# Four-layer diffusion backbone on one core: where the last layer's conditioning products run

## The chip, the core and the metric

The kernel runs on one core of a Trainium2 chip. Five engines work on instruction streams of their own: TensorE (PE, matmuls and transposes), VectorE (DVE), ScalarE (ACT), GpSimd (POOL) and SyncE (SP, which here only issues DMA transfers). Engines wait for one another by semaphores, and DMA queues move data between device memory and the on-chip buffers. The metric is device time in microseconds of one execution, as the median of several.

## The reference

Four layers run one after the other over 384 tokens: 128 context tokens and 256 latent tokens, each of width 1024. Layers 0 and 3 are S5 state-space mixers, layer 1 is a pooling mixer, layer 2 is latent attention (MLA). Each layer is normed, shifted and scaled by its conditioning, mixed, multiplied with a SiLU path z, projected back and added to the residual with a conditioned gate:

```python
def _ada(cond, w, b):
    m = jax.nn.silu(cond) @ w + b            # (1024) @ (1024, 3072)
    return jnp.split(m, 3, axis=-1)
for layer in range(4):
    sh, sc, g = _ada(c, ada_w[layer], ada_b[layer])    # and the same for c_ctx
    h = _rmsnorm(x, norm_g[layer]) * (1 + sc) + sh
    u, z = jnp.split(h @ w_in, 2, axis=-1)             # MLA: z beside q, ckv, kpe
    y = mixer(u)                                       # S5: scan over the tokens, then GLU
    x = x + g * ((y * silu(z)) @ w_out)
```

The conditioning (shift, scale and gate of every layer) depends on the two vectors c and c_ctx alone, so its products may run at any time before the layer that uses them.

## The kernel before

**Conditioning.** Each of the 4 layers has three parts: shift (part 0), scale (part 1) and gate (part 2). A part is a product of the two condition vectors with a 1024 x 1024 block of ada_w. `ada_steps` (from line 82) cuts a part into four steps. A step loads two 512 KB pieces of weights, `adw`, over SP's queue, and TensorE multiplies each piece in four fp32 matmuls on 32 columns (line 99), which the trace shows as 8 records. So a part is 8 loads and 64 records. The loads go into a ring named "araw" with two buffers (layer 0's shift and scale also use another ring). The sums stay in one PSUM bank, `adps`, of the pool `ad`, which has a single bank that other work shares. The last step adds the bias on VectorE (`adarow`, line 51 through a helper); then shift and scale are transposed on TensorE (`adt`, line 111) and written by ScalarE or VectorE, and a gate is stored by four small transfers (`gd`).

**Order of the parts.** `program` keeps all 48 steps in a list `todo`, in order of layer and part; `fill()` takes the next four, which is one part. Layer 0's shift and scale are done before its scan. The other ten parts, 40 steps with 80 loads, are all handed out in layer 0's scan.

**First scan (layer 0, `S5Body.run`).** The S5 layer works in four blocks b of channels. Per block TensorE makes the inputs u (line 213), chunk products (line 1122), a recurrence over time steps runs on VectorE (tiles Pr, E, R at line 51), ScalarE copies the states (`Eq`, lines 1185 and 1188, 2.9 us each), and TensorE makes the outputs from them (lines 1208 and 1212). z products of layer 0 (line 204) and the parts of the conditioning fill TensorE beside the recurrence; the lines are

```python
for k in range((3, 4, 3, 6)[b]):
    at(62, self.z, zs.pop(0))
if fill:
    for k in range((4, 3, 2, 1)[b]):
        at(45, fill)
```

so the four blocks get 4, 3, 2 and 1 parts: 32, 24, 16 and 8 loads.

**Attention layer (layer 2).** Its projection has 16 z products (`zprod`), each 24 matmuls of a 512 KB weight (lines 159 to 161), which ScalarE and VectorE first split in two (`whi` line 138, `wlo` line 51). After each, `side(1, 1)` is called: its first number runs one task of preparation of layer 3's tables (`S5Ahead`, which makes its tables P and t in the ring "araw" as well, and stores and loads them over SP), its second calls `fill(1)`, which finds `todo` empty.

**Later scan (layer 3, `S5Skewed.run`).** The same work in five phases f, with the tables loaded instead of made (`Wl`, ring "araw", asked for in phases 0 to 2), and its z products in three matmuls per tile (lines 159 to 161). The second half of the GLU work (lines 829 to 831) comes behind it.

**What sets the order.** The code hands instructions to a scheduler that arranges each engine's stream anew by when operands come ready, so the streams differ from the order of the code; each engine then runs its stream in order. A wait holds up all that stands behind it on the same engine or queue.

Of the kernel before, what the change touches and what calls it, by code (L numbers as in the profile page):

```python
# [9 lines left out]
F32 = mybir.dt.float32  # L10
# [20 lines left out]
class Net:  # L31
# [51 lines left out]
    def ada_steps(self, l, g):  # L83


        nc, m = self.nc, self.mods[l]
        st = {}

        def load(ks):
            if 0 in ks:  # L90
                st["ps"] = self.ad.tile([128, 256], F32, name="adps", tag="ad")
                st["row"] = self.load(self.work, self.A["ada_b"][l, g], [128, 256], "adarow", bufs=1)
            ps, first = st["ps"], l == 0 and g < 2
            for k in ks:
                tag = "raw" if first and k % 3 else "araw"
                raw = self.ring.tile([128, 4, 256], F32, name="adw", tag=tag, bufs=4 if tag == "raw" else 2)
                nc.sync.dma_start(raw, self.A["ada_w"][l, g, k])
                for h in range(4):
                    nc.tensor.matmul(ps[32 * h:32 * h + 32, :], self.scond[:, k, :], raw[:, h, :], start=k == 0, stop=k == 7)  # L99
            if 7 in ks:  # L100
                finish(ps, st["row"])

        def finish(ps, row):
            self.tt(row, ps, row, OP.add)
            if g == 2:
                for h in range(4):
                    nc.sync.dma_start(m["gd"][:, h * 256:(h + 1) * 256], row[32 * h:32 * h + 2, :])
                return
            pt = self.ad.tile([128, 2, 4, 32], F32, name="adt", tag="ad")
            for k in range(2):  # L110
                nc.tensor.transpose(pt[:, k].rearrange("p h c -> p (h c)"), row[:, k * 128:(k + 1) * 128], self.ident)
            pv = pt[:, :, :, 0:2].rearrange("p k h c -> p h k c")
            if g == 0:
                nc.scalar.copy(out=m["sh"].rearrange("p (h k) c -> p h k c", k=2), in_=pv)
            else:
                for k in range(2):
                    nc.vector.scalar_tensor_tensor(out=m["sc"][:, k::2, :], in0=pt[:, k, :, 0:2], scalar=1.0,
                                                   in1=self.gT[:, l, k::2].unsqueeze(2).broadcast_to([128, 4, 2]),
                                                   op0=OP.add, op1=OP.mult)

        return [lambda ks=range(i, i + 2): load(ks) for i in range(0, 8, 2)]
# [910 lines left out]
class S5Body:  # L1032
# [198 lines left out]
    def run(self, h, fill, glu):  # L1231
        self.h = h

        self.Es = [p.tile([128, 99, 64], F32, name="E", tag="e") for p in (self.eps[0], self.e1)]
        self.Ps, self.Ms = {}, {}
        self.u(0)
        for qq in range(4):
            self.win(0, qq)
        zs = list(range(16))
        for b in range(4):  # L1240
            tasks = {}
            at = lambda i, f, *a: tasks.setdefault(i, []).append(lambda: f(*a))
            if b < 3:
                at(4, self.u, b + 1)
            for qq in range(4):
                if b < 3:
                    at(8 + 14 * qq, self.win, b + 1, qq)
                at(6 + 14 * qq, self.mats, 4 * b + qq)
            for k in range((3, 4, 3, 6)[b]):
                at(62, self.z, zs.pop(0))  # L1250
            if fill:
                for k in range((4, 3, 2, 1)[b]):
                    at(45, fill)
            if b == 3:
                for q in range(8):
                    at(min(62, 30 + 6 * q), glu.early_y, self.wq, q)
                for q in zs:
                    at(62, self.z, q)
                for q in range(2):
                    at(62, glu.early_prod, q)  # L1260
            self.rec(b, tasks)
            for qq in range(4):
                q = 4 * b + qq
                self.out(b, qq)
                if b == 3:
                    for k in range(2, 6):
                        if (0, 1, 2, 3, 3, 3)[k] == qq:
                            glu.early_prod(k)
                if qq < 2:
                    self.Ms[q + 2] = self.m_mat(q + 2)  # L1270
        self.nc.sync.dma_start(self.A["o_s5"][self.j], self.fin.rearrange("p q g r -> p (q g r)"))


class S5Skewed(S5Body):
# [17 lines left out]
    def run(self, h, fill, glu):  # L1292
# [7 lines left out]
        for f in range(5):  # L1300
# [9 lines left out]
            for k in range((2, 4, 4, 5, 1)[f]):  # L1310
                at(14 + 3 * k, self.z, zs.pop(0))
            if f == 3:
                for q in range(8):
                    at(8 + 3 * q, glu.early_y, self.wq, q)
            if f == 4:
# [24 lines left out]
def program(tc, A, layers=(0, 1, 2, 3), final=True):  # L1340
    with ExitStack() as ctx:
# [28 lines left out]
        for l in layers:  # L1370
            n = [0, 0]

            def side(k, a):
                n[0] += k
                n[1] += a
                while ahead and n[0] >= 1:
                    ahead.side()
                    n[0] -= 1
                while n[1] >= 1:
                    fill(1)  # L1380
                    n[1] -= 1

            def end():
# [150 lines left out]
```

## Time and profile before

| | us |
|---|---|
| median of 3 runs | 1811.44 (1811.34 to 1813.9) |
| profiled execution, its own time | 1812.23 |
| its span | 1810.4 |
| TensorE busy in it | 1686.1 (93%) |
| mean granted TensorE clock | 0.963 of full |

The page gives the busy time of each engine and the chain of work that ended last. Other views cut the same execution finer: windows (busy time per engine in a stretch), waits (what ended the idle time of an engine), the chain in order of time, and timelines of single instructions, in which a number in brackets is the idle time before an instruction and what ended it. A row with x8 stands for 8 records of the same shape, back to back or overlapping, so the step from its start to the next row's start is what it holds the engine for.

### The profile page before, as it was taken

Reading aid. Unit: us, or ns where it says so; the run is one execution under the profiler, and the core shown is the slowest. Engines: PE = TensorE matmul, PEld = TensorE weight load, DVE = VectorE, ACT = ScalarE, POOL = GpSimd, SP = SyncE. Lnnn points to the kernel's source line nnn. Section 1 sums busy time; section 2 is a strip of 40 time slices with the busy share of each in tenths; the row PEclk is TensorE's granted clock in tenths of the full one; section 3 lists DMA queues with packets and bytes.
Section 4 is the critical chain, followed back from the end, with each engine's and each line's share of the span. In section 5 each row is a group of like instructions: output and inputs, shape, how many; then the busy total and the mean of one; then the engine's idle time right before and its main releaser. Section 6 shows DMA issues by size and latency. Waiting matters only on the chain.

```text
span 1810.4 us, 29493 instructions
## 1 busy us (share of the span) xinstructions
PE 1686.1 (93%) x10928; PEld 1318.4 (73%) x10928; DVE 1254.9 (69%) x3149; ACT 978.3 (54%) x1588; POOL 5.4 (0%) x16
## 2 busy tenths in 40 slices
PE   4999999998999998999998999999899999899998
PEld 1464454654799977999887885657678778689986
DVE  7699876787476567888867737763439978656435
ACT  2653487636654455655546555642354777754322
POOL 0000000000000000000000000000000000000000
PEclk7999999997899998999998999999999999799999
DMA  8337767654577664655563566732567754567552
GB/s 311 98 119 240 228 182 220 195 180 137 166 252 231 193 205 135 188 162 163 179 218 113 186 205 229 239 127 82 181 226 226 227 182 140 166 232 213 172 165 72
DMA packets 174831, 334.30 MB, mean 185 GB/s; under 512 B 78528, under 2 KB 101856, under 8 KB 174688
## 3 DMA queue, kind: packets, MB, share of 16 engines
q1 hardware_dynamic: 165728, 319.84, 55.6%
q10 hardware_dynamic: 8960, 12.59, 2.1%
q8 instruction: 86, 1.41, 0.3%
q14 instruction: 57, 0.47, 0.1%
HBM read 279.54 MB, written 52.82 MB: 184 GB/s over the span
## 4 chain that ended last, share of the span: by engine, by line
PE 72%; DVE 9%; ACT 9%; DMA 6%; issue 3%; SPq 0%; ACTq 0%; DVEq 0%
PE acc L175 6%; PE acc L177 6%; PE acc L176 6%; PE sp L1122 4%; PE acc L829 4%; PE acc L830 4%; PE acc L831 4%; PE acc L213 3%; PE acc L159 3%; PE acc L160 3%; PE acc L161 3%; PE acc L204 3%; ACT Eq L1188 3%; DMA adw<-in_ada_w 2%; PE adps L99 2%
## 5 line engine op out<-in xcount | busy, mean ns | idle before, releaser
L51 DVE TENSOR_TENSOR wlo<-raw,whi 128x1024 fp32r<-128x1024 f32 (+2 forms) x234 | 281.2, 1204 | 246.3 <-ACT whi L138 229.0
L138 ACT CAST whi<-raw 128x1024 fp32r<-128x1024 f32 x246 | 257.6, 1050 | 315.2 <-PE acc L177 130.0
L51 DVE TENSOR_TENSOR Pr<-E,Tb 128x256 f32<-128x256 f32 (+1 forms) x504 | 173.9, 354 | 9.3 <-ACT E L1131 3.3
L159 PE MATMUL acc<-hh,whi 128*128 128x384 f32 x512 | 177.3, 347 | 0.2
L161 PE MATMUL acc<-hh,wlo 128*128 128x384 f32 x512 | 174.3, 340 | 0.3 <-DVE wlo L51 0.2
L160 PE MATMUL acc<-hl,whi 128*128 128x384 f32 x512 | 174.3, 340 | 0.0
L829 PE MATMUL acc<-y,whi 128*128 128x384 f32 x448 | 152.7, 345 | 8.1 <-ACT y L146 5.8
L831 PE MATMUL acc<-y,wlo 128*128 128x384 f32 x448 | 152.0, 340 | 1.0 <-DVE wlo L51 1.0
L830 PE MATMUL acc<-y,whi 128*128 128x384 f32 x448 | 152.7, 342 | 0.1
L175 PE MATMUL acc<-whi,ph 128*128 128x512 f32 x384 | 152.5, 397 | 0.0
L176 PE MATMUL acc<-wlo,ph 128*128 128x512 f32 x384 | 151.4, 394 | 0.0
L177 PE MATMUL acc<-whi,pl 128*128 128x512 f32 x384 | 151.3, 394 | 0.0
L51 DVE TENSOR_TENSOR E<-R,E 128x128 f32<-128x128 f32 (+1 forms) x504 | 123.1, 254 | 31.5 <-ACT E L1125 25.2
L51 DVE TENSOR_TENSOR R<-Pr 128x128 f32<-128x128 f32 (+1 forms) x504 | 123.7, 255 | 5.8
L159 PEld LDWEIGHTS acc<-hh,whi 128*128 128x128 f32 x512 | 97.1, 190 | 5.2 <-issue 2.0
L204 PE MATMUL acc<-h,raw 128*128 128x384 f32 x256 | 98.8, 516 | 0.0
L161 PEld LDWEIGHTS acc<-hh,wlo 128*128 128x128 f32 x512 | 96.8, 189 | 2.1 <-DVE wlo L51 0.9
L160 PEld LDWEIGHTS acc<-hl,whi 128*128 128x128 f32 x512 | 97.1, 190 | 1.0 <-issue 0.3
L99 PE MATMUL adps<-adw,scond 128*32 128x256 f32 x768 | 70.6, 422 | 27.7 <-DMA adw<-in_ada_w 27.3
L213 PE MATMUL acc<-raw,h 128*128 128x512 f32 x192 | 95.8, 617 | 0.0
L829 PEld LDWEIGHTS acc<-y,whi 128*128 128x128 f32 x448 | 84.6, 190 | 11.6 <-ACT y L146 7.1
L831 PEld LDWEIGHTS acc<-y,wlo 128*128 128x128 f32 x448 | 84.9, 190 | 2.2 <-DVE wlo L51 1.6
(285 smaller groups left out, 3261.6 us busy)
## 6 DMA issues: line engine op xcount, KB each, us to landing
adw<-in_ada_w SPq DMA_DIRECT2D x96, 512.0 KB
raw<-in_s_glu SPq DMA_DIRECT2D x64, 512.0 KB
raw<-in_s_wu SPq DMA_DIRECT2D x48, 512.0 KB
raw<-in_s_wz SPq DMA_DIRECT2D x40, 512.0 KB
raw<-in_s_wo SPq DMA_DIRECT2D x32, 512.0 KB
yq<-yd SPq DMA_DIRECT2D x64, 192.0 KB
lod<-wlo SPq DMA_DIRECT2D x24, 512.0 KB
wlo<-lod SPq DMA_DIRECT2D x24, 512.0 KB
```

Of the source, the lines that this page charges most:

```text
L51: return self.nc.vector.tensor_tensor(out=out, in0=a, in1=b, op=op)
L138: nc.scalar.copy(out=hi, in_=raw)
L159: nc.tensor.matmul(ps, h, xh[:, kk, :ncol], start=i == 0, stop=False)
L160: nc.tensor.matmul(ps, h, xl[:, kk, :ncol], start=False, stop=False)
L161: nc.tensor.matmul(ps, l, xh[:, kk, :ncol], start=False, stop=i == n - 1)
L175: nc.tensor.matmul(ps, xh[:, kk, xs], h, start=kk == 0, stop=False)
L176: nc.tensor.matmul(ps, xh[:, kk, xs], l, start=False, stop=False)
L177: nc.tensor.matmul(ps, xl[:, kk, xs], h, start=False, stop=kk == 2 * nu - 1)
L204: self.nc.tensor.matmul(ps, w[:, k * 128:(k + 1) * 128], x[:, k, :], start=k == 0, stop=k == 7)
L829: self.nc.tensor.matmul(ps, h, y[:, 0, k], start=u == 0 and k == 0, stop=False)
L830: self.nc.tensor.matmul(ps, h, y[:, 1, k], start=False, stop=False)
L831: self.nc.tensor.matmul(ps, l, y[:, 0, k], start=False, stop=u == 1 and k == 7)
```

## The change

The last layer's three parts leave the first scan. The blocks now get 3, 2, 2 and 0 parts (24, 16, 16 and 0 loads). Shift and scale of layer 3, eight steps with 16 loads, are handed out one step after each of the first eight z products of the attention layer. The gate, four steps with 8 loads, is handed out in phase 3 of the later scan, and it sums in a bank of the pool `sp` instead of `ad`.

```diff
@@ ada_steps
         def load(ks):
             if 0 in ks:
-                st["ps"] = self.ad.tile([128, 256], F32, name="adps", tag="ad")
+                st["ps"] = (self.ad.tile([128, 256], F32, name="adps", tag="ad") if (l, g) != (3, 2) else
+                            self.bank(self.sp, "sp")[:, :256])
@@ S5Body.run
             if fill:
-                for k in range((4, 3, 2, 1)[b]):
+                for k in range((3, 2, 2, 0)[b]):
                     at(45, fill)
@@ S5Skewed.run
             if f == 3:
+                at(4, fill)
                 for q in range(8):
                     at(8 + 3 * q, glu.early_y, self.wq, q)
@@ program, side
                 while n[1] >= 1:
-                    fill(1)
+                    if l == 2 and todo and todo[0][:2] <= (3, 1):
+                        fill(1)
                     n[1] -= 1
```

Lines of the changed kernel are one higher from line 92 on (two from 1315, three from 1383): its line 100 is line 99 of before. The streams of the two kernels show the moves. In the next pieces a load of adw is one row with x4, its four matmuls.

TensorE, first scan, end of the first block: `L204` are layer 0's z products, `L1208` and `L1212` the block's outputs from the state copies Eq, `L214` (changed) the next block's inputs u. Before:

```order
L99 MATMUL adps<-adw,scond 32x256 x4
L204 MATMUL acc<-h,raw 128x384 x2
L99 MATMUL adps<-adw,scond 32x256 x4
L204 MATMUL acc<-h,raw 128x384 x3
L1212 MATMUL tp<-Eq,P 64x96 x4
L99 MATMUL adps<-adw,scond 32x256 x4
L1208 MATMUL tp<-U_608,M 128x96
L1212 MATMUL tp<-Eq,P 64x96 x4
```

Four more such loads stand in the eight rows ahead of it. Changed, at the same place:

```order
L112 MATMUL adt<-ident,adarow 128x128 x2
L214 MATMUL acc<-raw,h 128x512
L1209 MATMUL ad<-U_608,M 128x96
L214 MATMUL acc<-raw,h 128x512 x2
L205 MATMUL acc<-h,raw 128x384 x19
L1213 MATMUL tp<-Eq,P 64x96 x4
L1209 MATMUL tp<-U_608,M 128x96
L1213 MATMUL tp<-Eq,P 64x96 x4
```

These loads are gone, and 19 z matmuls stand together ahead of the first output.

SP's queue, layer 2's z products: `raw<-in_mla_wz` are the z weights; lfq, C, W, Td, Md, Pd and Wd are tables of layer 3's preparation. Before:

```order
L136 DMA raw<-in_mla_wz 128x1024
L1001 DMA Md_590<-W 128x512
L946 DMA Td_5190<-Tt 128x112
L55 DMA lfq<-Lfd_591 128x64
L136 DMA raw<-in_mla_wz 128x1024 x2
L991 DMA Wd_588<-W 128x1024
L994 DMA Pd_589<-P 128x1024
L136 DMA raw<-in_mla_wz 128x1024
```

Changed:

```order
L995 DMA Pd_589<-P 128x1024
L98 DMA adw<-in_ada_w 128x1024
L137 DMA raw<-in_mla_wz 128x1024
L98 DMA adw<-in_ada_w 128x1024
L947 DMA Td_5021<-Tt 128x112
L137 DMA raw<-in_mla_wz 128x1024 x3
L55 DMA adarow<-in_ada_b 128x256
L55 DMA lfq<-Lfd_591 128x64
L98 DMA adw<-in_ada_w 128x1024 x2
L992 DMA Wd_588<-W 128x1024
L137 DMA raw<-in_mla_wz 128x1024
```

Loads of adw and of the bias (adarow) now stand among the z weights and the preparation's transfers.

TensorE, later scan, phase 3: `L1208`, `L1212` (before) and `L1209`, `L1213` (changed) are the outputs from Eq, `L159` to `L161` (changed: `L160` to `L162`) the z products. Before:

```order
L1208 MATMUL tp<-U_12635,M 128x96
L1212 MATMUL tp<-Eq,P 64x96 x4
L1208 MATMUL ad<-U_12635,M 128x96
L159 MATMUL acc<-hh,whi 128x384
L160 MATMUL acc<-hl,whi 128x384
L161 MATMUL acc<-hh,wlo 128x384
L159 MATMUL acc<-hh,whi 128x384
```

Changed:

```order
L1209 MATMUL tp<-U_12579,M 128x96
L1213 MATMUL tp<-Eq,P 64x96 x4
L1209 MATMUL ad<-U_12579,M 128x96
L100 MATMUL sp<-adw,scond 32x256 x8
L160 MATMUL acc<-hh,whi 128x384
L161 MATMUL acc<-hl,whi 128x384
L162 MATMUL acc<-hh,wlo 128x384
```

Two loads (x8) of the gate stand ahead of the z matmuls that follow an output group; three more such pairs follow further down, the last of them 94 rows on, so that z matmuls move behind later outputs.

## Rows read from the trace of the kernel before

**Rows 1.** The page, parts 1 and 4.

```profile
PE 1686.1 (93%) x10928; PEld 1318.4 (73%) x10928; DVE 1254.9 (69%) x3149; ACT 978.3 (54%) x1588; POOL 5.4 (0%) x16
...
PE 72%; DVE 9%; ACT 9%; DMA 6%; issue 3%; SPq 0%; ACTq 0%; DVEq 0%
```

**Rows 2.** Windows: us; busy us of each engine (x instructions), granted clock, DMA share, GB/s.

```profile
90.00:457.00 367.00, 339.49 (x2836) 189.49 (x2832) 297.69 (x980) 211.11 (x309) 0.30 (x2) 0.96 0.60 187
...
1020.00:1080.00 60.00, 60.00 (x358) 55.77 (x351) 26.42 (x34) 30.62 (x51) 0.00 (x0) 1.00 0.64 201
1500.00:1600.00 100.00, 87.69 (x622) 74.73 (x621) 75.55 (x253) 75.84 (x62) 0.00 (x0) 0.90 0.54 177
```

**Rows 3.** Windows of the tile adps alone, first scan: PE, PEld, DVE, clock, DMA, GB/s.

```profile
90.00:457.00 367.00, 56.50 (x640) 15.42 (x640) 4.23 (x10) 0.96 0.60 187
```

**Rows 4.** TensorE's waits in the first scan: for whom, us, times, longest.

```profile
PE tp L1212 <- ACT Eq L1188: 9.9, 4, 4.5
PE adps L99 <- DMA adw<-in_ada_w: 8.5, 8, 2.4
```

**Rows 5.** Chain that ended last, shares by line: 90 to 460, then 430 to 460 us.

```profile
by line: PE acc L204 14.4%; PE acc L213 11.8%; PE sp L1122 10.4%; DMA adw<-in_ada_w 10.1%; PE adps L99 10.0%; ACT Eq L1188 6.2%; issue 5.2%; PE sp L910 3.2%; PE ad L1212 3.2%; ACT Eq L1185 3.1%; PE sp L938 2.8%; DVE Pr L51 2.5%; PE ad L1208
...
by line: PE acc L204 43.8%; DMA adw<-in_ada_w 15.9%; PE adps L99 14.5%; ACT Eq L1188 9.5%; PE tp L1212 5.7%; PE sp L938 4.2%; PE tp L1208 3.3%; ACT sz L1095 1.7%; ACTq L1097 1.1%; issue 0.8%; ACTq L1188 0.1%
```

**Rows 6.** Windows of shorter stretches, columns as in rows 2.

```profile
150.00:200.00 50.00, 47.56 (x294) 19.87 (x286) 43.97 (x191) 4.31 (x11) 0.00 (x0) 1.00 0.80 254
...
360.00:390.00 30.00, 29.98 (x175) 15.55 (x173) 28.38 (x139) 2.42 (x5) 0.00 (x0) 1.00 0.76 253
400.00:410.00 10.00, 10.00 (x74) 6.77 (x73) 3.21 (x6) 8.33 (x7) 0.00 (x0) 0.66 0.10 30
...
1080.00:1100.00 20.00, 18.31 (x76) 11.39 (x75) 16.44 (x40) 13.94 (x27) 0.00 (x0) 1.00 0.84 294
```

**Rows 7.** TensorE's timeline, first block's end: start, length, instruction, idle before.

```profile
205.83 0.64 PE L99 MATMUL adps<-adw,scond 128*32 128x256 f32 x8 [1.39 <-DMA adw<-in_ada_w]
...
209.17 0.64 PE L99 MATMUL adps<-adw,scond 128*32 128x256 f32 x8
209.74 1.56 PE L204 MATMUL acc<-h,raw 128*128 128x384 f32 x4
```

**Rows 8.** TensorE's timeline, fourth block, as rows 7.

```profile
435.96 1.08 PE L99 MATMUL adps<-adw,scond 128*32 128x256 f32 x8 [2.39 <-DMA adw<-in_ada_w]
436.97 4.21 PE L204 MATMUL acc<-h,raw 128*128 128x384 f32 x6
...
457.31 0.55 PE L1212 MATMUL tp<-Eq,P 128*64 128x96 f32 x8 [2.42 <-ACT Eq L1188]
```

**Rows 9.** Chain in order of time: start, length, what.

```profile
187.25 4.64 DMA adw<-in_ada_w
...
211.05 2.92 ACT Eq L1188
...
333.56 6.22 DMA adw<-in_ada_w
```

**Rows 10.** ScalarE's timeline beside the z products.

```profile
1056.42 1.05 ACT L138 CAST whi<-raw 128x1024 fp32r<-128x1024 f32 x1 [2.72 <-PE acc L160]
...
1060.58 1.05 ACT L138 CAST whi<-raw 128x1024 fp32r<-128x1024 f32 x1 [2.72 <-PE acc L160]
```

**Rows 11.** TensorE's timeline, layer 2: first transposes, last z product's end.

```profile
961.63 0.66 PE L267 MATMUL sp<-ident,xn 128*128 128x128 f32 x2 [4.31 <-issue]
...
1072.86 0.33 PE L161 MATMUL acc<-hh,wlo 128*128 128x384 f32 x1
```

**Rows 12.** TensorE's timeline, later scan.

```profile
1535.23 0.55 PE L1212 MATMUL ad<-Eq,P 128*64 128x96 f32 x8 [1.49 <-ACT Eq L1188]
...
1561.94 0.69 PE L829 MATMUL acc<-y,whi 128*128 128x384 f32 x1 [3.43 <-ACT y L146]
```

**Rows 13.** TensorE's timeline, third block's end.

```profile
399.52 0.55 PE L1212 MATMUL tp<-Eq,P 128*64 128x96 f32 x8 [3.00 <-ACT Eq L1188]
```

## Prediction, written before the changed kernel ran

> **What bounds the kernel now.** I read the page first. TensorE is busy 93% of the span and holds 72% of the chain that ended last [rows 1], so an instruction taken off TensorE counts wherever no other engine is just behind it, and one put on TensorE costs its full time wherever TensorE has no gap. The change moves work between three stretches, so the table by stretch comes next [rows 2]. In the first scan (90 to 457 us) TensorE is busy 339.49 of 367 us, VectorE 297.69 and ScalarE 211.11. In the stretch with the attention layer's z products (1020 to 1080) TensorE is busy 60.00 of 60, VectorE only 26.42. In the later scan (1500 to 1600) TensorE is busy 87.69 of 100 and ScalarE 75.84.
>
> The moved work is the conditioning. In the first scan its matmuls are 640 records, 80 loads of 8, 56.50 us busy [rows 3]. TensorE waits there for two things above all: 9.9 us for ScalarE's Eq copies and 8.5 us for conditioning weights (adw) [rows 4]. The chain says the same from the other side: 10.0% of the 370 us are adps matmuls and 10.1% adw transfers, 74 us together [rows 5]. So this stretch is mostly bound by TensorE's order and by its loads, with ScalarE second, and VectorE close in places (43.97 of 50 us at 150 to 200 us) [rows 6].
>
> **First scan: 24 of 80 loads leave.** By the blocks of the scan the loads go from 32, 24, 16, 8 to 24, 16, 16, 0. What one load costs on the path is the start of its 8 records to the start of the next matmul: 209.17 to 209.74, 0.57 us [rows 7]; at the low clock, 435.96 to 436.97, 1.01 us [rows 8]. The first 16 loads at 0.57 are 9.1 us. The last 8, of the fourth block, begin at the low clock and end at the high one; I take 0.75 each, between the two, 6.0 us. Waits that go with them: 1.39 us at 205.83 [rows 7], 2.39 us at 435.96 [rows 8], and of the rest a share, 8 of the 24 loads of the second block, about 1.3 us of those in [rows 4]. Sum 9.1 + 6.0 + 5.1 = 20.2 us.
>
> Not all of it comes out. At 208 to 219 us the chain runs on ScalarE's Eq copies (2.92 us each, [rows 9]) and not on TensorE; there the freed time is only filled by z products moved up from below, which is what the order shows for the first block's end. That pays later if TensorE is the limit later, which it is at 360 to 390 (29.98 of 30) [rows 6]. In the fourth block the chain goes over adw, adps and the z matmuls (15.9%, 14.5% and 43.8% of 30 us [rows 5]) into the Eq copy that TensorE waits for until 457.31 [rows 8], so there the relief is on the path. I take **-17 us**. The bounds: -8 (only the fourth block, 6.0 + 2.4) and -20.
>
> **z products: 16 loads are added.** One z product is 4.16 us (the weight split for one starts at 1056.42, for the next at 1060.58 [rows 10]), all of it TensorE, so 16 loads at 0.57 add 9.1 us. By the order the first two stand before layer 2's first transposes, where TensorE is idle 4.31 us [rows 11], and that gives back 2 x 0.57 = 1.1 us. Then the waits. A load's buffer comes free when TensorE has read it, the ring has two, and a round trip takes 4.64 us (187.25) to 6.22 us (333.56) [rows 9]. In the order the four loads from the third of the scale part on stand 9 or 10 z matmuls apart; two gaps and a load are 20 x 0.173 + 0.57 = 4.0 us (0.173 = 4.16 / 24), so a wait of 0.6 to 2.2 us comes up at two or three of them. At the densest place of the first scan (150 to 200 us) 18 loads left TensorE idle for 50 - 47.56 = 2.4 us [rows 6]. Here the DMA engines also carry the z weights (512 KB per 4.16 us, 126 GB/s) and layer 3's preparation, 201 GB/s in all [rows 2]. The loads stand from the idle at 961 to 82 z matmuls (14 us) before the last one at 1072.86 [rows 11]; 16 of 0.524 MB over these 98 us add 86 GB/s and make 287, about what the busiest slices show (294 GB/s at 1080 to 1100 [rows 6]). I take 3 us of waits: 9.1 - 1.1 + 3.0 = **+11 us**. Bounds: +8 (no wait) and +17 (every second load waits about 1.1 us). What queues behind: on TensorE the next z matmul; on SP the z weights and the preparation's stores, issued in order behind a load that waits for its buffer; on VectorE, behind the two adarow additions, which wait for a part's last load, the splits of z weights that TensorE reads next. VectorE has 33 of 60 us free here.
>
> The Trainium skill, "DMA: Bandwidth & Descriptors", section "Anatomy of one DMA", fits a transfer, for GpSimd's path, as about 2 us fixed plus its bytes over 436 GB/s. As an estimate from that page a 512 KB load takes 3.2 us, where the trace shows 4.64 to 6.22 for these loads of SP's queue; by the page the waits beside the z products would vanish and their term would be +8 instead of +11. The measured rows decide, so I keep +11.
>
> **Later scan: 8 loads are added.** 8 x 0.5 to 0.57 us is 4 to 4.6 us. They stand before ScalarE's Eq copies, where TensorE idles 1.49 us, with 3.43 us further on for y [rows 12]; they take the place of z matmuls, which slide into those gaps. The cover is ScalarE, 75.84 of 100 us [rows 2]. I take **+0.5 us**; without the cover it is +4.6, with one wait for a load (2.4 us, as at 435.96) +7; and -1 if the slid z matmuls fill gaps so that the clock, 0.90 over this stretch [rows 2], rises a little. The accumulator takes one of the two sp banks, but no other sp matmul stands between these loads in the order, so nothing waits for it. The four gd stores and adarow are the same in number as before.
>
> **Sum.** -17 + 11 + 0.5 = -5.5 us. Of the profiled run, 1812.23 us, that leaves 1806.7; the median shown is 0.8 us below the profiled run, so **1806.0 us**.
>
> **Rivals.**
> A, the first scan gives little. ScalarE's Eq copies and VectorE's recurrence (28.38 of 30 us at 360 to 390 [rows 6]) hold the scan where TensorE gets shorter. For it: the 9.9 us [rows 4]; against it: the 74 us of [rows 5]. The relief is then 9 to 13 us, the rest as above, net +2.5 to -1.5: 1810 to 1814, no measurable change.
> B, **slower**: the z products starve. The loads share SP, ring and DMA engines with the z weights and the preparation, which here are already at 201 GB/s; the ring's other users, the preparation's own tables, lengthen the round trip to the 6.22 us seen. If 8 of the 14 loads wait 1.3 us each, that is 10 us. Idle time of some us has cost clock in this trace: TensorE idled 3.00 us before 399.52 [rows 13], and from 400 to 410 us the granted clock is 0.66 [rows 6], a mix of its two levels, 2.4 and 1.2 GHz. One such 10 us here costs 3 to 4 us. Then z is +9.1 - 1.1 + 10 + 3 = +21, net +4.5 to +8 with a first scan of -17 to -13.5: 1816 to 1819. It decides from about 9 us of waits in the z stretch. For it: adw is what TensorE waits for in the first scan too, 8 times [rows 4], with no z weights beside it; against: from 1020 to 1080 TensorE has no gap at all at 201 GB/s [rows 2].
> The Trainium skill, "TensorE: Matmul & The Clock Gate", section "Part 1: The HAM clock gate", says that the engine is throttled unless it is kept active; the row at 399.52 agrees, and that is why B carries the clock term.
> C, all comes out: -20 in the first scan, its end at a higher clock too, z at +8, later scan -1: -13, 1798.
> D, the move changes what the scheduler does elsewhere so that gain and cost cancel (the order below the moved loads differs on all queues): about 1811.
>
> **Chances.** The forecast 0.38 (gain of 3.6 to 10 us, 1801 to 1807.8), A 0.22, B 0.25, C 0.08, D 0.07. A measurement of this kernel tells 0.2%, 3.6 us, from no change. Faster is forecast and C, 0.46; same is A and D, 0.29; slower is B, 0.25. The range reaches from half of C to two thirds of B: 1799 to 1819 leaves out about 0.04 + 0.08, and some 0.05 for sizes beyond all bounds.
>
> **What would show it.** In the changed profile: 56 loads of adw in 90 to about 440 us, no TensorE wait for adw near 205 and 435, and the scan's last copy 15 us earlier or more. Right in size if the layer 3 preparation's stretch (first transposes of layer 2 to the attention scores) is 9 to 13 us longer with at most 4 us of waits for adw. Wrong if TensorE's waits for Eq in the first scan grow from 9.9 us by over 8 (rival A), or if waits for adw or z weights near 1000 to 1060 exceed 9 us or the clock there falls below 1.00 (rival B). The later scan should hold its time within 1 us from layer 3's first Eq copy to its last.

## The result and the profile after

The changed kernel takes 1838.37 us (median of 4 runs, 1834.54 to 1838.95), the kernel before 1811.85 beside it: a ratio of 1.014, 95% interval 1.0124 to 1.0157. It is slower by 26.5 us, outside the range of 1799 to 1819. The profiled run took 1834.54 us with a span of 1832.6, 22.3 more than the profiled run of before; the comparisons of stretches below are of these two executions.

The page after, parts 1 and 4, against [rows 1] (from here on lines of the changed kernel are numbered one to three higher, as the change section says):

```profile
PE 1696.7 (93%) x10928; PEld 1325.2 (72%) x10928; DVE 1248.7 (68%) x3149; ACT 977.6 (53%) x1588; POOL 5.4 (0%) x16
...
PE 69%; DVE 10%; ACT 9%; DMA 8%; issue 3%; SPq 0%; ACTq 0%; DVEq 0%
```

TensorE is busy 10.6 us more, and its share of the last chain falls from 72% to 69% while the DMA's rises from 6% to 8%. Of the 22.2 us that the span grew, 10.6 are thus longer busy time for the same 10928 records, and 11.6 are idle time of TensorE. Windows after, columns as in [rows 2]:

```profile
90.00:457.00 367.00, 328.93 (x2655) 190.88 (x2651) 297.32 (x986) 214.10 (x314) 0.30 (x2) 0.92 0.52 156
1020.00:1080.00 60.00, 57.51 (x389) 47.90 (x388) 25.61 (x37) 25.98 (x46) 0.00 (x0) 1.00 0.73 226
1500.00:1600.00 100.00, 91.95 (x754) 77.69 (x753) 78.38 (x268) 78.09 (x74) 0.00 (x0) 0.94 0.63 204
```

In the first scan's 367 us TensorE is busy 328.93 us against 339.49, so it did get lighter. But VectorE is busy 297.32 against 297.69 us, and TensorE's granted clock fell from 0.96 to 0.92. Where TensorE got its time back it waited. Its waits after, in the stretch of [rows 4]:

```profile
PE tp L1213 <- ACT Eq L1189: 22.0, 4, 11.8
PE adps L100 <- DMA adw<-in_ada_w: 5.6, 11, 1.0
```

The wait for Eq is 22.0 us where it was 9.9. The wait for adw shrank from 8.5 to 5.6. What was taken off TensorE came back as waiting for ScalarE's copies. These in turn wait for the last step of VectorE's recurrence (`E`). ScalarE's timeline shows it for the third block, before and then after:

```profile
393.73 2.89 ACT L1185 COPY Eq<-E 64x1536 f32<-64x1536 f32 x1 [17.70 <-DVE E L51]
```

```profile
395.01 2.83 ACT L1186 COPY Eq<-E 64x1536 f32<-64x1536 f32 x1 [0.51 <-DVE E L51]
```

In the kernel before too, ScalarE stood idle until the recurrence was done, 17.70 us there. With less work on TensorE the recurrence ended no earlier. In the timeline of TensorE, and in a window of the stretch:

```profile
400.72 0.91 PE L1213 MATMUL tp<-Eq,P 128*64 128x96 f32 x8 [11.76 <-ACT Eq L1189]
```

```profile
395.00:430.00 35.00, 23.12 (x160) 16.93 (x163) 21.94 (x69) 28.59 (x18) 0.00 (x0) 0.50 0.10 29
```

The first wait was 3.00 us before [rows 13]; it is 11.76 now, and over this window the granted clock is 0.50, the lower of its two levels (1.2 GHz), where the same window had 0.68 before and 400 to 410 had 0.66 [rows 6].

How far the changed kernel is ahead (-) or behind (+) along the program, by the start of the same instruction in both profiles (us), with four experiments beside it. Eq and the norms are ScalarE's copies and norms:

| mark | before | after | relief alone | no gate | no shift, scale | own ring |
|---|---|---|---|---|---|---|
| first scan, second block's first Eq | 272.95 | -1.2 | -3.1 | -0.4 | -1.9 | +1.3 |
| third block's first Eq | 393.73 | +1.3 | +2.9 | +4.4 | +2.7 | +6.8 |
| fourth block's first Eq | 454.40 | +0.2 | +1.8 | +3.2 | +1.6 | +5.1 |
| layer 1, first norm (xn) | 695.59 | -5.1 | -4.1 | -1.3 | -3.2 | -1.3 |
| layer 2, first norm (xn) | 962.12 | -3.9 | -1.1 | +0.2 | -0.3 | 0.0 |
| layer 2, first scores (mx) | 1077.58 | +15.2 | -1.8 | +17.8 | +0.2 | +11.0 |
| layer 3, first norm (xn) | 1306.74 | +15.5 | -0.4 | +18.1 | +0.3 | +12.4 |
| layer 3, second block's Eq | 1482.48 | +15.2 | -4.0 | +18.1 | +0.2 | +9.4 |
| layer 3, last Eq but one | 1607.54 | +18.2 | -3.4 | +17.6 | +0.2 | +10.0 |
| end of TensorE's stream | 1802.5 | +22.2 | +1.4 | +17.2 | +3.1 | +16.1 |

So the first scan gives 5.1 us where 17 were forecast, the stretch of the z products costs 19.1 where 11 were, and the later scan with what follows 6.7 where 0.5 was. Layer 1, in which nothing was moved, loses 1.2 of the 5.1 again, and the rest of layer 2 takes 0.3.

Layer 2's start shows how the z stretch turns bad. TensorE first, then VectorE, after:

```profile
953.32 0.64 PE L100 MATMUL adps<-adw,scond 128*32 128x256 f32 x8
957.86 1.06 PE L100 MATMUL adps<-adw,scond 128*32 128x256 f32 x2 [3.90 <-DMA adw<-in_ada_w]
958.85 0.69 PE L268 MATMUL sp<-ident,xn 128*128 128x128 f32 x2
959.47 1.07 PE L100 MATMUL adps<-adw,scond 128*32 128x256 f32 x6
960.47 0.69 PE L268 MATMUL sp<-ident,xn 128*128 128x128 f32 x2
962.68 0.69 PE L268 MATMUL sp<-ident,xn 128*128 128x128 f32 x2 [1.52 <-DVE xn L258]
```

```profile
960.60 0.69 DVE L51 TENSOR_TENSOR P<-C,lfq 128x512 f32<-128x512 f32 x1 [2.08 <-PE adps L100]
961.21 0.15 DVE L247 SCALAR_TENSOR_TENSOR rs<-rt,rs 128x1 f32<-128x1 f32 x1
961.28 0.68 DVE L51 TENSOR_TENSOR P<-C,lfq 128x512 f32<-128x512 f32 x1
961.88 0.74 DVE L258 TENSOR_SCALAR xn<-x,rs 128x1024 f32<-128x1024 f32 x1
```

The 4.31 us of idle in [rows 11] were counted as cover for two loads. The second of them arrives late, TensorE waits 3.90 us for it, and its 8 records end only at 960.47. Until then it holds a buffer of the ring "araw". VectorE's next product of layer 3's preparation (`P<-C,lfq`) needs that buffer and waits 2.08 us for `adps L100`; behind it in VectorE's queue stand `rs` and `xn`, the norm of layer 2, for which TensorE then waits 1.52 us. The norm began 3.9 us early; at the first z product 1.0 us of that lead is left (it starts at 983.61, before at 984.64). So layer 2's start costs 2.9 of the 19.1 us.

The other 16.1 us come between the z products, where the remaining 14 loads stand. TensorE there, after:

```profile
1069.69 0.34 PE L161 MATMUL acc<-hl,whi 128*128 128x384 f32 x1
1069.87 0.34 PE L162 MATMUL acc<-hh,wlo 128*128 128x384 f32 x1
1070.14 0.64 PE L100 MATMUL adps<-adw,scond 128*32 128x256 f32 x8
1070.71 0.45 PE L160 MATMUL acc<-hh,whi 128*128 128x384 f32 x1
1070.99 0.34 PE L161 MATMUL acc<-hl,whi 128*128 128x384 f32 x1
```

From start to start a z matmul holds TensorE 0.17 to 0.18 us (1069.69 to 1069.87), a load's 8 records 0.57 us, but the z matmul before the load 0.27 and the one behind it 0.28. A load among z matmuls therefore costs 0.77 us, not 0.57. It is the same in the first scan of the kernel before, where layer 0's z matmuls hold TensorE 0.32 us among themselves, 0.42 ahead of the load at 209.17 [rows 7] and 0.43 behind it. By an estimate from these rows the 14 loads take about 11 us; TensorE's waits for adw between them are 4.1 us in four places, and about 1 us is left.

### The profile page after: what moved, and what is told of

Its sections match the earlier page's. It is cut to its first block, busy times and chain, and to the rows that moved or that the text cites. A ratio compares the mean times of both kernels' runs of the same rounds, so it can differ in the third digit from the quotient of the medians.

```text
span 1832.6 us, 29501 instructions
## 1 busy us (share of the span) xinstructions
PE 1696.7 (93%) x10928; PEld 1325.2 (72%) x10928; DVE 1248.7 (68%) x3149; ACT 977.6 (53%) x1588; POOL 5.4 (0%) x16
## 4 chain that ended last, share of the span: by engine, by line
PE 69%; DVE 10%; ACT 9%; DMA 8%; issue 3%; SPq 0%; ACTq 0%; DVEq 0%
PE acc L178 6%; PE acc L177 6%; PE acc L176 6%; PE sp L1123 4%; PE acc L830 4%; DMA adw<-in_ada_w 4%; PE acc L831 4%; PE acc L832 4%; PE acc L160 3%; PE acc L161 3%; PE acc L162 3%; PE acc L214 3%; ACT Eq L1189 3%; PE adps L100 2%; PE sp L731 2%
## 5 line engine op out<-in xcount | busy, mean ns | idle before, releaser
L160 PE MATMUL acc<-hh,whi 128*128 128x384 f32 x512 | 177.4, 347 | 0.3 <-ACT whi L139 0.2
L51 DVE TENSOR_TENSOR Pr<-E,Tb 128x256 f32<-128x256 f32 (+1 forms) x504 | 170.1, 351 | 7.8 <-ACT E L1132 2.5
L161 PE MATMUL acc<-hl,whi 128*128 128x384 f32 x512 | 175.3, 342 | 0.0
L162 PE MATMUL acc<-hh,wlo 128*128 128x384 f32 x512 | 174.6, 341 | 0.2 <-DVE wlo L51 0.2
L51 DVE TENSOR_TENSOR E<-R,E 128x128 f32<-128x128 f32 (+1 forms) x504 | 119.1, 251 | 33.7 <-ACT E L1126 28.2
L51 DVE TENSOR_TENSOR R<-Pr 128x128 f32<-128x128 f32 (+1 forms) x504 | 119.7, 252 | 5.2
L160 PEld LDWEIGHTS acc<-hh,whi 128*128 128x128 f32 x512 | 96.8, 189 | 7.7 <-issue 4.6
L161 PEld LDWEIGHTS acc<-hl,whi 128*128 128x128 f32 x512 | 97.0, 189 | 4.2 <-issue 3.5
L162 PEld LDWEIGHTS acc<-hh,wlo 128*128 128x128 f32 x512 | 96.9, 189 | 2.3 <-issue 0.8
L205 PE MATMUL acc<-h,raw 128*128 128x384 f32 x256 | 94.4, 511 | 2.7 <-ACT sz L1096 2.7
L100 PE MATMUL adps<-adw,scond 128*32 128x256 f32 x704 | 68.4, 437 | 29.4 <-DMA adw<-in_ada_w 28.9
L214 PE MATMUL acc<-raw,h 128*128 128x512 f32 x192 | 94.9, 614 | 0.0
```

Of the source, the lines that this page charges most:

```text
L51: return self.nc.vector.tensor_tensor(out=out, in0=a, in1=b, op=op)
L160: nc.tensor.matmul(ps, h, xh[:, kk, :ncol], start=i == 0, stop=False)
L161: nc.tensor.matmul(ps, h, xl[:, kk, :ncol], start=False, stop=False)
L162: nc.tensor.matmul(ps, l, xh[:, kk, :ncol], start=False, stop=i == n - 1)
L214: self.nc.tensor.matmul(ps, x[:, kk, T * 128:(T + 1) * 128], w[:, k * 512:(k + 1) * 512], start=kk == 0, stop=kk == 7)
```

## The experiments

Two theories are tried against the prediction's own steps. **Theory 1**: the first scan is paced by VectorE's recurrence and the Eq copies behind it, so lightening TensorE there gains little. **Theory 2**: about half of what the z stretch pays comes from the ring that adw shares with the preparation.

In all of these the first scan of the changed kernel keeps its 3, 2, 2, 0 parts unless the diff says otherwise; each is a small edit of one of the two kernels. "Bias alone" is this edit of `ada_steps`, with other conditions on layer and part; `finish` then leaves out the addition of the sums:

```diff
         def load(ks):
+            if (l, g) in ((3, 0), (3, 1), (3, 2)):
+                if 7 in ks:
+                    finish(None, self.load(self.work, self.A["ada_b"][l, g], [128, 256], "adarow", bufs=1))
+                return
...
```

### What the first scan gives back, nothing put elsewhere

The diff above, on the changed kernel.

> The changed kernel, with the products of layer 3's conditioning left out (24 loads and 192 records; shift, scale and gate are made from the bias alone): what the first scan gives back when nothing is put elsewhere. Theory 1 (the first scan is paced by VectorE's recurrence and ScalarE's Eq copies, TensorE only waits longer): 5 us below before, about 1807. Rival (the prediction's step, 17 us of the loads lie on the path and the loss comes elsewhere): about 1795.

Measured: 1813.49 us, before 1811.77 on the same chip, ratio 1.001 (0.9993 to 1.0028). Leaving the 24 loads out altogether gains nothing that can be measured over the whole kernel; in the profile it is 4.1 us ahead at layer 1's norm, and it loses 4.8 us behind the last Eq but one, where nothing of the change stands (the last section shows how). Over the six profiles with this first scan (after, this one, no gate, no shift and scale, own ring, one load) the lead at that mark is 5.1, 4.1, 1.3, 3.2, 1.3 and 0.8 us, 2.6 in the mean, and at layer 2's norm 0.5 in the mean. Theory 1 held for the scan, and even its 5 us were too many. By this run no other place for these three parts should make the kernel faster by more than these few us, as long as the scan is dealt this way; that is argued from the run, other places were not tried.

### The gate's price

The same edit for (3, 2) alone, on the changed kernel.

> The changed kernel, with the 8 loads and 64 records of layer 3's gate left out of the later scan (gate from the bias alone). Theory 1 (the gate's loads are on the path there): 4 to 7 us below the changed kernel, 1831 to 1834. Rival (the prediction's step, ScalarE covers them): within 1.5 us of the changed kernel, 1837 to 1838.5.

Measured: 1829.14 us, 9.2 below the changed kernel. (The changed kernel was not run again beside these experiments; the kernel before was, and lay at 1811.77 here.) In the table the two run in step up to layer 3's norm (2.6 us apart) and differ by 7.6 us more at the end. Theory 1 held, with a price above its range.

### The price of shift and scale beside the z products

The same edit for (3, 0) and (3, 1).

> The changed kernel, with the 16 loads and 128 records of layer 3's shift and scale left out of the stretch of the z products (both from the bias alone). Theory 1 (the z stretch pays for records, waits for adw and for the held-up first transposes): 17 to 20 us below the changed kernel, about 1819. Rival (the prediction's term): 11 us below, about 1827.

Measured: 1815.13 us, 23.2 below the changed kernel; the stretch from layer 2's norm to its first scores is 116.0 us, 134.6 in the changed kernel and 115.5 before. So the whole excess of this stretch, 18.6 us, hangs on these 16 loads. Theory 1 held, with a price above its range.

### The gate alone

On the changed kernel, with the first scan dealt so that the gate alone is left over; beside the z products nothing is then handed out, as in the kernel before.

```diff
-                for k in range((3, 2, 2, 0)[b]):
+                for k in range((4, 3, 2, 0)[b]):
```

> The kernel before with the gate alone moved to the later scan (blocks of the first scan with 4, 3, 2, 0 parts), all else as before. By the prediction's steps the fourth block's 8 loads are on the path, 8.4 us, and the later scan takes 0.5: about 1804. Theory 1 (scan paced by the other engines, gate's loads on the later path): relief 3, price 4 to 7, 1813 to 1816.

Measured: 1818.39 us, 6.6 above before, ratio 1.0034 (1.0018 to 1.0051). The prediction's fourth block is refuted: the 8 loads are gone from it, and at layer 1's norm the kernel is 0.8 us behind; Theory 1's relief of 3 us did not come either, and its 1813 to 1816 was missed. The chain of this kernel, at the end of the fourth block:

```profile
459.84 0.24 DVE R L51
460.14 0.40 issue
460.53 1.23 DVE wlo L51
462.14 1.22 DVE wlo L51
463.74 1.22 DVE wlo L51
465.12 0.24 DVE E L51
465.44 2.85 ACT Eq L1189
```

The fourth block's first Eq copy starts at 465.44, in the kernel before at 454.40. TensorE's freed time drew the next stage forward: splits of GLU weights (`wlo`, 1.22 us each) now stand in VectorE's queue between the last steps of the recurrence (R and E here), and the chain runs over them. The relief was real on TensorE and was spent on VectorE, in front of what everyone waits for. The kernel before had little to give at this place in any case. VectorE's timeline, before:

```profile
452.72 0.23 DVE L51 TENSOR_TENSOR E<-R,E 128x64 f32<-128x64 f32 x1
452.98 1.53 DVE L1185 COPY Eq<-E 64x1536 f32<-64x1536 f32 x1
```

The recurrence ended at 452.95, and ScalarE's Eq copy began at 454.40: it could have begun 1.5 us earlier at most, however little TensorE had to do.

### Own buffers for shift and scale

On the changed kernel.

```diff
+            self.adz = hctx.enter_context(tc.tile_pool(name="adz", bufs=1, side="right"))
...
-                raw = self.ring.tile([128, 4, 256], F32, name="adw", tag=tag, bufs=4 if tag == "raw" else 2)
+                raw = (self.adz if l == 3 and g < 2 else self.ring).tile([128, 4, 256], F32, name="adw", ...)
```

> The changed kernel, but layer 3's shift and scale load into two buffers of their own instead of the ring that the preparation of layer 3's tables uses too. Theory 2 (of the z stretch's price, about half is waits that come from the shared ring, on TensorE for adw and at layer 2's start through VectorE's preparation product that waits for a buffer): 7 to 10 us below the changed kernel, about 1829. Rival (the DMA engines and SP's queue are the limit there, the ring is not): within 3 us of the changed kernel, 1835 to 1839.

Measured: 1828.32 us, 10.0 below the changed kernel, and 1.0074 times before (1.0049 to 1.0098). The stretch is 126.5 us instead of 134.6. TensorE's wait for adw in it, after and here:

```profile
PE adps L100 <- DMA adw<-in_ada_w: 8.0, 5, 3.9
```

```profile
PE adps L100 <- DMA adw<-in_ada_w: 4.2, 3, 3.3
```

From 8.0 to 4.2 us, of which 3.3 stand ahead of the norm; between the z products 0.9 is left of 4.1. Layer 2's start, up to the first z product, costs 0.5 us instead of 2.9. The remaining 2.5 us or so go with the order: three loads instead of two stand ahead of the first z product, and several of the others run in pairs. Theory 2 held: sharing the ring with the preparation is about two fifths of this stretch's price. The rival's range missed, but 11.0 us of the price are left without the sharing.

### Records without loads

On the changed kernel: a part loads its first piece only and multiplies it eight times.

```diff
+                own = l == 3 and g < 2
+                if not own or k == 0:
+                    raw = (self.adz if own else self.ring).tile([128, 4, 256], F32, name="adw", ...)
                     nc.sync.dma_start(raw, self.A["ada_w"][l, g, k])
+                    st["raw"] = raw
+                raw = st["raw"]
```

> The changed kernel with 2 of the 16 loads of the z stretch: each of the two parts loads one piece of weights into a buffer of its own and multiplies it eight times, so that all 128 records run and 14 loads are left out. What the records alone cost. Theory 2: the stretch from layer 2's norm to its first attention scores is 8 to 10 us longer than before instead of 19, total about 1827. Rival (records are covered, the loads cost all): 1820 or less.

Measured: 1820.35 us (1810.75 to 1831.49), and 117.6 us for the stretch, 2.1 more than before; counted from layer 1's norm to the scores, 4.8 more. (The profiled execution, 1828.93 us, is one of the slower ones.) Both expectations missed, the truth lies nearer to the rival. TensorE's timeline at layer 2's start:

```profile
959.10 3.66 PE L104 MATMUL adps<-adw,scond 128*32 128x256 f32 x64
963.49 0.41 PE L272 MATMUL sp<-ident,xn 128*128 128x128 f32 x2 [0.72 <-PE adps L104]
```

With nothing to wait for, 64 of the 128 records run in one piece of 3.66 us (0.46 us for 8) in the place of the idle time of [rows 11], and the transposes behind them wait only 0.72 us. The idle time was cover for records, as the prediction said, but not for loads. This run does not tell what the records cost in the changed kernel, though: with nothing to wait for, 90 of the 128 records stand ahead of the first z product, where the changed kernel has 16, and its other 112 stand between z products at the price read above. It tells that the records are cheap, 2 to 5 us, where they can be gathered ahead of the stage.

### The first scan without any conditioning

On the kernel before: bias alone for all ten parts that it handles in the scan (`if l or g == 2`).

> The kernel before with the products of all ten parts of the first scan left out (80 loads and 640 records; shift, scale and gate come from the bias alone). What the conditioning costs the first scan as a whole. Theory 1 (VectorE's recurrence and the Eq copies pace the scan): at most 20 us below before, 1792 to 1812. Rival (the prediction's reading, 80 loads of 0.57 us and 8.5 us of waits on the path): about 54 us below, 1758.

Measured: 1789.29 us, 24.4 below before, ratio 0.9863 (0.9828 to 0.9898). Theory 1's bound of 20 was a little short, the rival's 54 far off. The 80 loads cost 0.3 us each, not 0.57 with waits on top. Window of the third block's recurrence in this kernel:

```profile
332.00:388.00 56.00, 34.02 (x166) 20.73 (x164) 53.65 (x252) 14.06 (x17) 0.00 (x0) 0.82 0.24 69
```

TensorE is busy 34.02 of 56 us, and VectorE 53.65 of 56: the recurrence's operations follow one another. With the conditioning gone, they are what is left to limit the first scan's middle.

### A lighter recurrence, with and without the 24 loads

In layer 0's `step`, the middle one of the three VectorE operations is left out and its result replaced by a slice of Pr; once on the kernel before, once on the kernel that leaves layer 3's products out.

```diff
-        yield n.tt(rv.rearrange("p s a o -> p o s a"), pv[:, :, :, :, 0], pv[:, :, :, :, 1], OP.add)
+        if self.ahead:
+            yield n.tt(rv.rearrange("p s a o -> p o s a"), pv[:, :, :, :, 0], pv[:, :, :, :, 1], OP.add)
+        else:
+            R = P[:, 0]
```

> The kernel before, with the middle one of the three VectorE operations of each recurrence step of layer 0 left out (R<-Pr, 252 records, 63.6 us of VectorE in the first scan). Theory 1 (the recurrence on VectorE paces the first scan in its dense parts): 15 to 40 us below before. Rival (the prediction's reading, TensorE and its loads pace it): within 10 us of before.

> The changed kernel with layer 3's conditioning products left out (as in the run that measures what the first scan gives back), and the same VectorE operation of layer 0's recurrence left out. If VectorE is what swallowed the relief, taking 24 loads from the first scan now pays: 8 to 17 us below the trimmed kernel before. Rival (something else holds the scan, such as the Eq copies or the blocks' transfers): within 4 us of it.

Measured: 1794.71 us (1790.21 to 1795.20, 4 runs) with the loads and 1781.73 us (1780.79 to 1790.94, 4 runs) without them, before 1811.56. Window with the loads:

```profile
90.00:457.00 367.00, 344.33 (x2926) 192.41 (x2923) 268.54 (x743) 225.71 (x322) 1.90 (x3) 0.98 0.63 192
```

With VectorE at 268.54 us in place of 297.69 (the window is fixed in time, so that it also holds work that was drawn into it), the same 24 loads are worth 13.0 us of the median (9.9 of the mean), and 16.4 us at layer 1's norm (13.5 and 30.0 ahead of before). That is close to the prediction's 17, in a kernel with more room on VectorE. With the full recurrence it is 2.6. Theory 1 is shown from both sides as far as VectorE goes. The edit takes out VectorE time and a link of the recurrence at once, so it does not tell which of the two counts, and ScalarE's Eq copies were not made lighter by any run.

### Other ways to deal the ten parts

On the kernel before: (3, 3, 3, 1), then (3, 3, 2, 2), instead of (4, 3, 2, 1).

> The kernel before with the ten parts dealt 3, 3, 3, 1 over the four blocks instead of 4, 3, 2, 1; nothing leaves the first scan. Theory 1 (the first block gives back most per load, 9 us for 32, and the third is paced by VectorE with little room): 0 to 3 us below before. Rival (the third block's TensorE is full at 360 to 390 us): 3 to 8 us above.

> The kernel before with the ten parts dealt 3, 3, 2, 2. Theory 1 (the first block pays for its loads, the fourth hides them): 0 to 4 us below before. Rival (the prediction's reading, the fourth block's loads are on the path at 1 us each): 3 to 6 us above.

Measured: 1816.60 us, before 1811.56, ratio 1.0019 (0.9991 to 1.0047), no clear difference, though the median lies 5.0 above, within the rival's 3 to 8, and Theory 1's 0 to 3 below did not come; and 1829.65 us, 1.0087 (1.0056 to 1.0117). Theory 1's expectation for the second missed badly, and the rival's 3 to 6 us too. The fourth block has no room for a second part. TensorE's timeline in it:

```profile
466.87 0.64 PE L99 MATMUL adps<-adw,scond 128*32 128x256 f32 x8 [2.51 <-DMA adw<-in_ada_w]
...
484.80 0.64 PE L99 MATMUL adps<-adw,scond 128*32 128x256 f32 x8 [0.39 <-DMA adw<-in_ada_w]
485.99 0.46 PE L1208 MATMUL ad<-U,M 128*128 128x96 f32 x2 [0.18 <-DVE adarow L51]
```

The added part spills behind the scan into the GLU stage. There TensorE waits up to 2.51 us for adw, and the last load and the addition of its part's bias (adarow) stand ahead of the output matmuls (L1208): the kernel goes from 6.6 us ahead at the fourth block's second Eq to 17.1 behind at layer 1's norm. Neither of the two beats the kernel before, and no other run with all of the computation in it does either.

## Why the prediction was wrong, point by point

**What bounds the scan.** This reading failed first. [rows 4] and [rows 5] were taken as 74 us of adps and adw on the path. A chain shows one longest way; it does not say how far behind the next one is. Here the next one was VectorE, whose 297.69 of 367 us in [rows 2] and 43.97 of 50 us in [rows 6] stood in the very rows that were read. With all 80 loads gone only 24.4 us are gained. In the fourth block, where the chain went over adw, adps and z matmuls, VectorE's recurrence ended just 1.5 us before that chain reached the Eq copy.

**First scan, -17.** The term measured 2.6 us of gain in the mean of six profiles (-5.1 in the one after), outside its bounds of -8 to -20. The step that failed is "which it is at 360 to 390 (29.98 of 30)": TensorE was full there beside a VectorE that was nearly full as well (28.38 of 30), and with less to do it only waited longer. The bound of -8 rested on the fourth block, where the relief "is on the path"; the gate-alone run shows no gain there (0.8 us behind at layer 1's norm), since the freed time let GLU splits go ahead of the recurrence on VectorE. The price per load, 0.57 us, was not what failed here: with its neighbours a load costs 0.77, and with the lighter recurrence 24 loads give 10 to 16.4 us.

**z products, +11.** It measured +19.1, above the bound of +17. Three terms of the sum were too small. The records (9.1 - 1.1 = 8.0 us) went by 0.57 us a load, which leaves out what the load does to its neighbours; with them it costs 0.77, so that 14 loads take about 11. The waits were 3 us; between the z products they measured 4.1. And the idle time ahead of layer 2's transposes was counted as a gain, where the load that came late to it cost 2.9 us. The forecast's own term counted a round trip per buffer of a ring that adw has to itself. The ring is shared with the preparation's tables (B named that, as a longer round trip of the loads), and a buffer held by a late load stops VectorE's preparation product and with it the norm queued behind. The two adarow additions were named as VectorE's only new wait, and the wait that mattered, for a buffer, was not seen. By the run with buffers of its own the sharing is 8 of the 19 us; that is another cut through the same 19, and not to be added to the terms above.

The Trainium skill's estimate from "DMA: Bandwidth & Descriptors", section "Anatomy of one DMA" (3.2 us for 512 KB, on GpSimd's path), would have made the term smaller still. This case does not bear it out for SP's loads: [rows 9] have 4.64 and 6.22 us for one, and the waits for adw beside the z products did not vanish but measured 4.1 us.

**Later scan, +0.5.** It measured 7.6 us (changed kernel against the one without the gate's products, from layer 3's norm to the end), near its bound of +7, by luck: that bound held one wait of 2.4 us for a load, and TensorE waits 0.7 us for adw here. The cover did not come. About 3.5 us come in the scan itself, from its second block's Eq to the last Eq but one, where the gate's loads stand as four pairs that hold TensorE 1.0 to 1.9 us each, and 4.4 behind it, where no load of the gate is any more. TensorE's timeline at the last outputs, then the window of 50 us from the last Eq but one; after:

```profile
1626.85 0.55 PE L1213 MATMUL tp<-Eq,P 128*64 128x96 f32 x8 [2.68 <-ACT Eq L1189]
```

```profile
1626.00:1676.00 50.00, 45.66 (x296) 40.11 (x297) 18.96 (x29) 23.38 (x31) 0.00 (x0) 0.83 0.57 164
```

Before, at the same place:

```profile
1608.67 0.55 PE L1212 MATMUL tp<-Eq,P 128*64 128x96 f32 x8 [0.47 <-ACT Eq L1188]
```

```profile
1608.00:1658.00 50.00, 47.63 (x346) 42.61 (x345) 23.96 (x36) 25.71 (x34) 0.00 (x0) 1.00 0.65 195
```

The wait for Eq grows from 0.47 to 2.68 us, and the clock of this stretch falls from 1.00 to 0.83. In all five profiles with the gate's loads in the later scan this wait for Eq is 1.71 to 2.69 us, the clock of the 50 us 0.79 to 0.86, and the time from the last Eq but one to the end 197.9 to 201.1 us. Of the eight without them, six wait 0.44 to 0.60 us, at 1.00, and take 194.1 to 195.4. The other two (relief alone, and its twin with the light recurrence) wait 1.89 and 2.04 us and have 0.86 and 0.93.

What makes this wait stands on VectorE. Ahead of the last steps of the recurrence its queue has a `y`, which needs ScalarE's y, which needs a transfer, `yq`. ScalarE and VectorE after, then VectorE before:

```profile
1618.81 0.51 ACT L147 CAST y<-yq 128x384 fp32r<-128x384 f32 x1 [4.43 <-DMA yq<-yd]
...
1619.36 0.56 DVE L51 TENSOR_TENSOR y<-yq,y 128x384 fp32r<-128x384 f32 x1 [2.60 <-ACT y L147]
1619.83 0.22 DVE L51 TENSOR_TENSOR R<-Pr 128x64 f32<-128x64 f32 x1
```

```profile
1603.97 0.55 DVE L51 TENSOR_TENSOR y<-yq,y 128x384 fp32r<-128x384 f32 x1
```

After, VectorE idles 2.60 us for it, and the recurrence stands behind; before, it does not idle. It is so in all 13 profiles: the seven with the long wait for Eq have VectorE idle 1.45 to 4.83 us before this `y`, the six others under 0.2 us. So a transfer that lands late holds the recurrence, the recurrence holds Eq, and the low clock goes with the wait. The gate's loads bring it about each time, but not they alone; why the transfer is late in these seven was not found. This is read from the timelines; no run moved the transfer by itself.

**The rivals.** A and, in number, B came together: A's mechanism for the first scan, at a smaller relief than its 9 to 13 us, and B's number for the z products, +19.1 near its +21, though not by B's mechanism. B wanted 8 of 14 loads to wait 1.3 us each and the clock to fall; four loads wait 4.1 us in all between the z products, and by the prediction's own sign for B (over 9 us of waits near 1000 to 1060, or a clock below 1.00) it did not come: there it is 3.0 us at 1.00. That the sum came near was luck. The sign for A did come: the waits for Eq grew by 12.1 us, where over 8 was to show it. The prediction gave A and B as alternatives and worked out B with the forecast's own relief of 13.5 to 17; A and B at once would have given +8.5 to +12.5 from its own numbers (-13 to -9, +21 and +0.5). C and D did not come. B's clock term did not appear where it was expected: from 1020 to 1080 us the clock is 1.00 with TensorE busy 57.51 of 60 us. It appeared in the first scan and behind the later one.

**Sum by the runs.** -2.6 + 19.1 + 7.6 = 24.1 us, against 22.3 between the two profiles and 26.5 between the medians. The two profiles alone give -5.1 + 1.2 + 19.1 + 0.3 + 6.7 = 22.2, with layer 1 and the rest of layer 2 as the second and fourth term.

## What to carry to other kernels

Before work is counted as relief on an engine, look at what the engine beside it does in the same slices: where two engines are both nearly full, as here at 29.98 and 28.38 of 30 us, taking work from one moves the wait to the other, and a run that leaves the work out altogether tells it in one step. Price a moved instruction with its neighbours: a load's own records held TensorE 0.57 us here, but its place between z matmuls cost 0.77. Idle time of TensorE ahead of a layer's first transposes was cover here for matmuls whose data was there, not for loads that had to arrive; put ahead of the stage's own instructions they turned into a wait. When moved loads use a ring that another engine's work allocates from, follow who asks for that buffer next, and what is queued behind that request.

## What the runs showed of the hardware

The time of the kernel before scattered more than its first three runs said: on one chip 25 runs lay between 1804.95 and 1816.35 us, so the 0.2% (3.6 us) taken as the resolution is about the scatter of a single run; on another chip 15 runs reached from 1806.27 to 1826.38.

A load's 8 records on 32 columns made their neighbours slower by 0.1 us each: layer 2's z matmuls beside them hold TensorE 0.27 and 0.28 us, where it is 0.17 to 0.18 among themselves, and layer 0's 0.42 and 0.43, where it is 0.32.

A wait of about 2 us can have an outsized price through the clock. The kernel that leaves layer 3's products out has no gate loads in the later scan, and TensorE's order there is the same as before; yet it waited 1.89 us for the last Eq but one's outputs (VectorE had idled 1.45 us for the late `y`), and the clock went down:

```profile
1605.22 0.55 PE L1218 MATMUL tp<-Eq,P 128*64 128x96 f32 x8 [1.89 <-ACT Eq L1194]
```

```profile
1600.00:1605.00 5.00, 3.33 (x19) 3.01 (x18) 4.11 (x11) 2.35 (x3) 0.00 (x0) 1.00 0.75 230
1605.00:1618.00 13.00, 12.78 (x86) 10.38 (x87) 3.43 (x4) 8.26 (x8) 0.00 (x0) 0.55 0.51 159
```

From 1605 to 1618 us it is at 0.55 of full, where it had been at 1.00 up to that wait; the end came 4.8 us later against before than the last Eq but one. The Trainium skill, "TensorE: Matmul & The Clock Gate", section "Part 1: The HAM clock gate", says that the engine is throttled unless it is kept active; the rows agree in direction.

Cover can be large even in a kernel whose TensorE is busy 93% of the time: 80 loads and 640 records, 56.50 us of TensorE's busy time [rows 3], cost the whole kernel 24.4 us.
